# Two sums of weight quarters in a hybrid decoder block: from VectorE adds to adding transfers issued by GpSimd

## The chip, the cores and the metric

The kernel runs on one core of a Trainium2 chip. The metric is the device time of one execution in microseconds; lower is better. Five engines work side by side, each through its own queue in order: TensorE (PE; its weight loads are listed apart as PEld), VectorE (DVE), ScalarE (ACT), GpSimd (POOL) and SyncE (SP), which here issues most transfers between DRAM and the on-chip buffers. Semaphores tie the queues together.

## The reference, cut to what matters

One layer on 528 tokens (16 meta tokens and 512) of width 1024. The same normalised input `h` is projected by columns of one wide matrix `w_in`; a forgetting-attention (FoX) branch with 8 heads and an mLSTM branch with 4 heads are gated, merged and projected:

```
h = rms_norm(x, g_pre)
z = h @ w_in
(fq, fk, fv, ff, fz, mqk, mv, mi, mf, mo, mz, ga, gb) = split(z)
oa = forgetting_attention(fq, fk, fv, log_sigmoid(ff + b_fox_f))
ya = (oa * silu(fz)) @ w_a
...                                  # mLSTM branch: hb
yb = (hb * silu(mz)) @ w_b
merged = sigmoid(ga) * ya + sigmoid(gb) * yb
out = x + rms_norm(merged @ w_o, g_post)
```

All is float32. A matrix product is made from high and low parts of both factors (three products: high by high, high by low, low by high).

## The kernel before, in words

The four mLSTM heads come first, up to about 481 us of the profile; then the FoX branch in four pairs `p` of heads, with the gates `ga` and `gb` between them; then the merge and the output projection, from about 835 us.

Many projections are computed 256 columns at a time as a *unit* (`st_unit`) by a seven-product scheme on quarters: the weight block of 1024 rows by 256 columns is cut into quarters of 512 rows by 128 columns, the tokens likewise (`TB`, made once). Seven products of sums of quarters (X, Y, Z, W in `st_products`) take the place of eight. The unit's weights are made ready by `st_narrow`:

- SP loads two blocks of 512 KB: `r0` (rows 0 to 511) and `r1` (rows 512 to 1023). In each, `a` is the left 128 columns and `b` the right. They take two of the four buffers of the tag `raw`, which all weight loads of the kernel share in turn.
- The *a split*: the left half of `r0` (quarter a11) is split by `split` into a high part (ScalarE, L250) and a low part (VectorE, L252).
- VectorE adds in place: L263, left half of `r0` += right half of `r0` (the sum s3); L264, right half of `r0` += right half of `r1` (the sum s1).
- The *b split* of all of `r0` (s3 and s1), the *c split* of `r1` (a12 and a22), two more adds into `r1` (L269, L270: s2 and s4), and the *d split* of `r1`.

TensorE takes them in the order a (X), b (Y, Z), c (W, Y), d (X, Z), 12 matmuls each. In the profile a split's tiles are named after the unit and the letter: `wgb2b_h` and `wgb2b_l` are the high and low part of the b split of unit 2 of gate `gb`; its raw buffers appear as `wgb_r`. The units through `st_narrow` are: `mz` (8, in the mLSTM part) and, in the FoX part, `fq`, `fz`, `ga` and `gb`, 4 each, 16 in all. The projections `fk` (plain) and `fv` (`v_seven`, through `st_wide`) use other code.

Around them, `prob_part(p, m, ...)` makes one head's attention: TensorE makes scores `pl` in four row blocks; GpSimd adds a mask into a row of `ab` (L993); VectorE takes scores and `ab` to `lt` with the row minima `mn` (L1008), which frees the scores' bank; ScalarE exponentiates (L1013); VectorE inverts the row sum `rsum` (L1014); GpSimd (L1016) and VectorE (L1018) write the normalised row to `pn`. The tag of `lt` has two buffers. `ptr_part` transposes `pn` on TensorE (`pt`, `pmt`) and splits the result (`pth`, `ptl` at L1043 and L1044, `ptm`); `fout_part` multiplies by the values (`pfo`). `gb_part` multiplies `yb` by the gate on GpSimd (L974) and stores it through GpSimd's transfer queue (L975), which is all that queue carries.

The program is written in this order of parts, but a scheduler orders each engine's queue by its own estimates and places the semaphores; the order is fixed when the kernel is built. `behind` and `pin` hold a few instructions in place.

Of the kernel before, what the change touches and what calls it, by code (L numbers as in the profile page):

```python
# [12 lines left out]
ALU = mybir.AluOpType  # L13

P = 128
# [11 lines left out]
MV = 512  # L27
# [5 lines left out]
C_MO, C_MZ, C_GA, C_GB = 8208, 10256, 12304, 13328  # L33
# [20 lines left out]
def tile_hybrid_block(ctx: ExitStack, tc: tile.TileContext, x, meta, norm_pre, norm_post, w_in, b_fox_f,  # L54
                      conv_w, conv_b, b_i, b_f, g_head, w_a, w_b, w_o, out):
    nc = tc.nc
    V, S, G, T = nc.vector, nc.scalar, nc.gpsimd, nc.tensor
    x2, out2 = x[0], out[0]
    win, wa, wb, wo = w_in[0], w_a[0], w_b[0], w_o[0]
# [12 lines left out]
    def banks(name, n):  # L72

        return [psum1(f"{name}_{i}") for i in range(n)]
# [23 lines left out]
    def sb(shape, dt, tag, name, pool=None, **kw):  # L98

        n = 1  # L100
        for d in shape[1:]:
            n *= d
        size = BYTES.get(tag, 4096)
        t = (pool or wk).tile([shape[0], size // (2 if dt == BF16 else 4)], dt, tag=tag, name=name, **kw)[:, 0:n]
        if len(shape) == 3:
            t = t.rearrange("p (a b) -> p a b", a=shape[1])
        elif len(shape) == 4:
            t = t.rearrange("p (a b c) -> p a b c", a=shape[1], b=shape[2])
        return t
# [13 lines left out]
    def wload(src, k0, nk, c0, nc_, name):  # L123
        raws = []
        hk = 1024 // nc_
        for u in range(nk // hk):
            raw = wp.tile([P, hk, nc_], F32, tag="raw", bufs=4, name=f"{name}_r{u}")
            r0 = k0 + u * hk * P
            nc.sync.dma_start(raw, src[r0:r0 + hk * P, c0:c0 + nc_].rearrange("(k p) n -> p k n", p=P))
            raws.append(raw)  # L130
        return raws, hk, nc_, name
# [17 lines left out]
    def mm3(ps, ah, al, bh, bl, start, stop, **kw):  # L149
        T.matmul(ps, ah, bh, start=start, stop=False, **kw)  # L150
        T.matmul(ps, ah, bl, start=False, stop=False, **kw)  # L151
        T.matmul(ps, al, bh, start=False, stop=stop, **kw)  # L152
# [93 lines left out]
    def split(src, name, tags=("whi", "wlo"), pool=None, bufs=None, into=None):  # L246
        kw = {} if bufs is None else {"bufs": bufs}
        shape = [P, src.shape[1], src.shape[2]]
        hi = into[0] if into else (pool or wp).tile(shape, F32R, tag=tags[0], name=f"{name}_h", **kw)
        first = S.activation(hi, src, AF.Copy)  # L250
        lo = into[1] if into else (pool or wp).tile(shape, F32R, tag=tags[1], name=f"{name}_l", **kw)
        V.tensor_tensor(lo, src, f(hi), ALU.subtract)  # L252
        split.first = first
        return hi, lo

    def st_narrow(c0, name, into=None, late=None, first=None):

        (r0,), (r1,) = (wload(win, 512 * i, 4, c0, 256, f"{name}{i}")[0] for i in range(2))
        a, b = slice(0, P), slice(P, 2 * P)
        o = {"a11": split(r0[:, :, a], f"{name}a", ("whs", "wls"), mw, 1, into)}  # L260
        if first:
            behind(split.first, first)
        V.tensor_tensor(r0[:, :, a], r0[:, :, a], r0[:, :, b], ALU.add)  # L263
        V.tensor_tensor(r0[:, :, b], r0[:, :, b], r1[:, :, b], ALU.add)  # L264
        x, y = split(r0, f"{name}b")
        o["s3"], o["s1"] = (x[:, :, a], y[:, :, a]), (x[:, :, b], y[:, :, b])
        x, y = split(r1, f"{name}c")
        o["a12"], o["a22"] = (x[:, :, a], y[:, :, a]), (x[:, :, b], y[:, :, b])
        d = V.tensor_tensor(r1[:, :, b], r0[:, :, a], r1[:, :, b], ALU.add)  # L269
        V.tensor_tensor(r1[:, :, a], r1[:, :, a], r1[:, :, b], ALU.add)  # L270
        x, y = split(r1, f"{name}d")
        if late:
            behind(d, late[0])
            behind(split.first, late[1])
        o["s4"], o["s2"] = (x[:, :, a], y[:, :, a]), (x[:, :, b], y[:, :, b])
        return o
# [18 lines left out]
    def st_products(o, units, between=lambda i: None):  # L295


        begun = set()

        def prod(d, w, t):  # L300
            (wh_, wl_), (th, tl) = o[w], TB[t]
            for m, (wz, yx, _, ts) in enumerate(units):
                bank = wz if d in "WZ" else yx
                dst = bank[:, 0:256] if d in "WY" else bank[:, 256:512]
                first = (m, d in "WZ") not in begun
                begun.add((m, d in "WZ"))
                for k in range(4):
                    st, sp = first and k == 0, k == 3
                    if ts is None:
                        mm3(dst, wh_[:, k, :], wl_[:, k, :], th[:, k, :], tl[:, k, :], st, sp, skip_group_check=True)  # L310
                    else:
                        mm3(dst, th[:, k, ts], tl[:, k, ts], wh_[:, k, :], wl_[:, k, :], st, sp, skip_group_check=True)

        def halves(bank):
            return bank.rearrange("p (s n) -> p s n", s=2)

        prod("X", "a11", "b11")
        prod("Y", "s3", "t3")
        for wz, yx, snap, _ in units:
            S.activation(snap[:, 0:2], halves(yx), AF.Copy)  # L320
        between(0)
        prod("Z", "s1", "t1")
        prod("W", "a12", "b21")
        for wz, yx, snap, _ in units:
            S.activation(snap[:, 3], wz[:, 256:512], AF.Copy)
        prod("Y", "a22", "t4")
        between(1)
        prod("X", "s2", "t2")
        for wz, yx, snap, _ in units:
            st_products.copied = S.activation(snap[:, 2], yx[:, 256:512], AF.Copy)  # L330
        prod("Z", "s4", "b22")
        for wz, yx, snap, _ in units:
            V.tensor_tensor(yx[:, 256:512], snap[:, 0], yx[:, 256:512], ALU.subtract)
            V.tensor_tensor(halves(yx), halves(yx), snap[:, 2:4], ALU.subtract)
        for wz, yx, snap, _ in units:
            last = V.tensor_tensor(halves(wz), halves(wz), snap[:, 1:3], ALU.add)
        return last
# [33 lines left out]
    def behind(ins, other):  # L371

        tc.add_manual_dep(ins.ins, other.ins.name, mybir.DependencyInfo(
            mybir.DependencyClass.NoSync, mybir.DependencyReason.DATA), reason="behind")
        return ins
# [264 lines left out]
    a = gi  # L640
# [7 lines left out]
    for c in range(NCH):  # L648
        k0, k1 = NM + c * P, NM + (c + 1) * P
# [4 lines left out]
    for c in range(NCH):  # L654
        k0, k1 = NM + c * P, NM + (c + 1) * P
# [140 lines left out]
        mo_part.late = late  # L796
        return so

    def st_unit(c0, name, room, into=None, late=None, first=None):

        ps = banks(f"p{name}", 2)
        st_unit.added = st_products(st_narrow(c0, f"w{name}", into, late, first),
                                    [(ps[0], ps[1], room.rearrange("p a (b n) -> p (a b) n", b=2), None)])
        return ps

    def mz_part(h, u):
        g = sb([P, 2, SEQ], F32, ("qk1h", "qk1l")[u], f"gz{h}{u}")
        into = None
        if u:
            t = sb([P, 2, 4, P], F32R, "sg", f"wz{h}{u}a", gp)  # L810
            into = t[:, 0], t[:, 1]
        ps = st_unit(C_MZ + h * MV + u * 256, f"z{h}{u}", g, into, mo_part.late if h and not u else None)
        for m in range(2):
            mz_part.late = st_unit.added, S.activation(g[:, m, :], ps[m], AF.Sigmoid)
        for m in range(2):
            mi = 80 + h * 4 + u * 2 + m
            V.scalar_tensor_tensor(g[:, m, :], ps[m], gc[:, mi:mi + 1], g[:, m, :], ALU.mult, ALU.mult)
        return g
# [70 lines left out]
    for h in range(MH):  # L889
# [5 lines left out]
        k = conv_part(h, 1)  # L895
        if h:
            w = decay(h)
        if pend is not None:
            wb_part(pend[0], bt)
        if h == 0:  # L900
            v = v0
            ps = banks("pv01", 2)
# [4 lines left out]
            w = decay(0)  # L907
# [29 lines left out]
    def fk_part(p):  # L937
        w = wchunk(win, 0, KC, C_FK + p * 256, 256, f"wfk{p}")
        kh = sb([P, 2, L], F32R, "qk1h", f"fkh{p}")
        kl = sb([P, 2, L], F32R, "qk1l", f"fkl{p}")  # L940
        for m in range(2):
            ps = banks(f"pfk{p}{m}", 2)
            proj_t_all(ps, w, m)
            for u in range(2):
                hv = kh[:, m, u * HL:u * HL + HL]
                S.activation(hv, ps[u][:, 0:HL], AF.Copy)
                V.tensor_tensor(kl[:, m, u * HL:u * HL + HL], ps[u][:, 0:HL], f(hv), ALU.subtract)
        return kh, kl
# [130 lines left out]
    k = fk_part(0)  # L1079
# [3 lines left out]
    for p in range(FH // 2):  # L1083
        if p:
# [3 lines left out]
            k = fk_part(p)  # L1088
# [40 lines left out]
    for u in range(4):  # L1129
# [20 lines left out]
        if u < 2:  # L1150
            for i in range(2):
                b = 2 * u + i
# [11 lines left out]
    w = wchunk(wo, 0, KC, 0, 512, "wo_0")  # L1164
# [8 lines left out]
    for u in (2, 3):  # L1173
        w = wchunk(wo, 0, KC, u * 256, 256, f"wo{u}")
        for b in range(NCH):
            ps = psum1(f"pout{u}{b}")
# [40 lines left out]
```

## Time and profile before

| | |
|---|---|
| three runs | 928.32, 928.46, 929.09 us (median 928.46) |
| the profiled execution | 927.63 us, its span 925.8 us |
| TensorE, VectorE, ScalarE, GpSimd busy | 906.0, 730.4, 504.5, 117.5 us |
| TensorE's granted clock over the span | 0.999 |
| bytes by transfer | 97.54 MB; SP's queue 92.76 MB, GpSimd's queue 2.10 MB |

The span runs from the first to the last instruction. Busy times are of one execution; matmuls overlap each other and their ends are modelled, so a wait of TensorE is best read from the list of waits. A row of the timeline gives the start in us, the duration in us, engine, line, operation, output and inputs, and in brackets how long the engine had been idle before it and what ended that. A row of waits gives the engine and what waited, for whom, and then the sum in us, the number of times and the longest.

### The profile page before, as it was taken

To read this page: it belongs to the slowest core of one execution; us is meant where nothing else is said; L and a number is where in the kernel's file an instruction comes from. 1 tells how busy PE (TensorE), PEld (TensorE's weight loads), DVE (VectorE), ACT (ScalarE), POOL (GpSimd) and SP (SyncE) were. 2 spreads that over 40 slices of the span, in tenths; PEclk is the share of its full clock that TensorE was granted. 3 is DMA by queue.
4 is the path that set the end of the run, shared out by engine and by line. 5 is a ranking of instruction groups with operands and counts; after the bars stand their busy time and mean duration, and the time that the engine had idled before them with its cause. 6 is when DMAs were issued, how large, how long until landed. Compare 5 with 4: busy or idle time off the path is not lost.

```text
span 925.8 us, 16722 instructions
## 1 busy us (share of the span) xinstructions
PE 906.0 (98%) x6744; PEld 858.4 (93%) x6744; DVE 730.4 (79%) x1196; ACT 504.5 (54%) x860; POOL 117.5 (13%) x168
## 2 busy tenths in 40 slices
PE   8999899999999999999999999999999999999997
PEld 6998799899998999999999989999999999988887
DVE  6889688579887598876898866997896997985534
ACT  5646556545665456664565525565755665863231
POOL 3052000100101000000100002221333121300000
PEclk9999999999999999999999999999999999999999
DMA  7313143123331333231242442344342333258402
GB/s 233 94 50 103 46 134 91 40 69 92 117 112 57 92 91 90 95 103 51 95 114 69 124 128 73 95 123 137 100 142 81 102 112 121 87 203 300 140 18 91
DMA packets 78664, 97.54 MB, mean 105 GB/s; under 512 B 5237, under 2 KB 66773, under 8 KB 78586
## 3 DMA queue, kind: packets, MB, share of 16 engines
q1 hardware_dynamic: 76520, 92.76, 32.5%
q0 software_dynamic: 576, 2.10, 0.6%
q10 hardware_dynamic: 1490, 1.61, 0.5%
q8 instruction: 53, 0.87, 0.4%
q14 instruction: 25, 0.20, 0.1%
HBM read 90.62 MB, written 5.83 MB: 104 GB/s over the span
## 4 chain that ended last, share of the span: by engine, by line
PE 66%; DVE 22%; ACT 5%; issue 3%; DMA 2%; POOL 1%; DVEq 0%; POOLq 0%; ACTq 0%
PE pyb L151 3%; PE pyb L150 3%; PE pyb L152 3%; PE pz L150 3%; PE pz L152 3%; PE pz L151 3%; PE pqk L150 3%; PE pqk L152 3%; PE pqk L151 3%; PE pv L152 2%; PE pv L150 2%; PE pv L151 2%; PE pfk L150 2%; PE pfk L152 2%; PE pfk L151 2%
## 5 line engine op out<-in xcount | busy, mean ns | idle before, releaser
L151 PE MATMUL pyb<-bl,wb_h 128*128 128x512 f32 x128 | 49.8, 389 | 0.0
L152 PE MATMUL pyb<-bh,wb_l 128*128 128x512 f32 x128 | 49.8, 389 | 0.0
L150 PE MATMUL pyb<-bh,wb_h 128*128 128x512 f32 x128 | 49.8, 389 | 0.0
L1016 POOL TENSOR_SCALAR pn<-lt,rsum 128x128 f32<-128x128 f32 x32 | 30.4, 952 | 127.6 <-DVE rsum L1014 127.5
L732 DVE SCALAR_TENSOR_TENSOR y<-z,gc,y 128x512 f32<-128x512 f32 (+1 forms) x48 | 35.9, 754 | 2.1 <-ACT y L725 1.4
L150 PE MATMUL pfk<-hh,wfk_h 128*128 128x264 f32 x128 | 36.4, 285 | 0.0
L150 PE MATMUL pqk<-hh,wq_h 128*128 128x258 f32 x128 | 36.4, 284 | 0.0
L150 PE MATMUL pqk<-hh,wk_h 128*128 128x264 f32 x128 | 36.3, 284 | 0.0
L151 PE MATMUL pfk<-hl,wfk_h 128*128 128x264 f32 x128 | 36.3, 283 | 0.0
L152 PE MATMUL pqk<-hh,wk_l 128*128 128x264 f32 x128 | 36.3, 283 | 0.0
L152 PE MATMUL pfk<-hh,wfk_l 128*128 128x264 f32 x128 | 36.3, 283 | 0.0
L151 PE MATMUL pqk<-hl,wk_h 128*128 128x264 f32 x128 | 36.2, 283 | 0.0
L152 PE MATMUL pqk<-hh,wq_l 128*128 128x258 f32 x128 | 36.0, 282 | 0.0
L151 PE MATMUL pqk<-hl,wq_h 128*128 128x258 f32 x128 | 36.0, 282 | 0.0
L849 POOL TENSOR_TENSOR mrs<-mss,mhalf 128x1 f32<-128x1 f32 x16 | 9.2, 575 | 191.1 <-DVE mss L847 188.2
L993 POOL TENSOR_TENSOR ab<-ab,mask_q 128x128 f32<-128x128 f32 x32 | 27.0, 874 | 49.5 <-DVE vl L488 34.8
L144 DVE TENSOR_TENSOR wo_l<-wo_r,wo_h 128x1024 fp32r<-128x1024 f32 x12 | 15.7, 1313 | 16.9 <-ACT wo_h L142 16.9
L152 PEld LDWEIGHTS pyb<-bh,wb_l 128*128 128x128 f32 x128 | 24.0, 188 | 5.0
L150 PEld LDWEIGHTS pyb<-bh,wb_h 128*128 128x128 f32 x128 | 24.0, 188 | 4.9
L151 PEld LDWEIGHTS pyb<-bl,wb_h 128*128 128x128 f32 x128 | 24.0, 188 | 4.8
L884 DVE TENSOR_TENSOR yb<-pyb,yb 128x512 f32<-128x512 f32 x24 | 16.5, 686 | 13.9 <-PE pyb L152 13.9
L142 ACT ACTIVATE wo_h<-wo_r 128x1024 fp32r<-128x1024 f32 x12 | 12.7, 1059 | 24.4 <-PE pya L151 13.2
(2206 smaller groups left out, 3961.2 us busy)
## 6 DMA issues: line engine op xcount, KB each, us to landing
wv_r<-in_w_in_dram SPq DMA_DIRECT2D x16, 512.0 KB, 4.3
wo_r<-in_w_in_dram SPq DMA_DIRECT2D x16, 512.0 KB, 3.8
wz_r<-in_w_in_dram SPq DMA_DIRECT2D x16, 512.0 KB, 3.7
wb_r<-in_w_b_dram SPq DMA_DIRECT2D x16, 512.0 KB, 3.8
ab<-d_na SPq DMA_DIRECT2D x8, 672.0 KB, 4.5
wq_r<-in_w_in_dram SPq DMA_DIRECT2D x8, 512.0 KB, 3.7
wk_r<-in_w_in_dram SPq DMA_DIRECT2D x8, 512.0 KB, 3.6
wfq_r<-in_w_in_dram SPq DMA_DIRECT2D x8, 512.0 KB, 3.7
```

The source lines that it names most:

```text
L142: pin(S.activation(hi, raw, AF.Copy))
L144: pin(V.tensor_tensor(lo, raw, f(hi), ALU.subtract))
L150: T.matmul(ps, ah, bh, start=start, stop=False, **kw)
L151: T.matmul(ps, ah, bl, start=False, stop=False, **kw)
L152: T.matmul(ps, al, bh, start=False, stop=stop, **kw)
L732: V.scalar_tensor_tensor(y[:, t0:L], z[:, m, t0 + j:L + j], gc[:, j * 16 + mi:j * 16 + mi + 1], y[:, t0:L], ALU.mult, ALU.add)
L849: G.tensor_tensor(rs, ss, mhalf, ALU.pow)
L884: V.tensor_tensor(dst, ps[i], dst, ALU.add)
L993: G.tensor_tensor(ab[:, o:o + P], ab[:, o:o + P], mask_q, ALU.add)
L1016: G.tensor_scalar(pn[:, o:o + P].rearrange("p (g t) -> p g t", g=4), lt[:, 0:32].unsqueeze(1).to_broadcast([P, 4, 32]), rsum, None, ALU.mult)
```

## The change

In 16 of the 24 units, those of the FoX part, the sums s3 and s1 are no longer made by VectorE from `r0` and `r1`. GpSimd issues four transfers from DRAM, 256 rows by 128 columns each, that add the right quarters of `w_in` into `r0` in place: two into its right half (`b`, from rows 512 on) and then two into its left half (`a`, from rows 0 on). The right half needs only the load of `r0`; the left half also needs the a split to have read a11. The b split waits for all four. The mLSTM's `mz` units keep the adds.

```
-    def st_narrow(c0, name, into=None, late=None, first=None):
+    def st_narrow(c0, name, into=None, late=None, first=None, fetched=True):
...
-        V.tensor_tensor(r0[:, :, a], r0[:, :, a], r0[:, :, b], ALU.add)
-        V.tensor_tensor(r0[:, :, b], r0[:, :, b], r1[:, :, b], ALU.add)
+        if fetched:
+
+            for dst, k0 in ((b, 512), (a, 0)):
+                for i in range(2):
+                    rows = win[k0 + 256 * i:k0 + 256 * i + 256, c0 + P:c0 + 2 * P]
+                    G.dma_start(r0[:, 2 * i:2 * i + 2, dst], rows.rearrange("(k p) n -> p k n", p=P), accum_op=ALU.add)
+        else:
+            V.tensor_tensor(r0[:, :, a], r0[:, :, a], r0[:, :, b], ALU.add)
+            V.tensor_tensor(r0[:, :, b], r0[:, :, b], r1[:, :, b], ALU.add)
...
-    def st_unit(c0, name, room, into=None, late=None, first=None):
+    def st_unit(c0, name, room, into=None, late=None, first=None, fetched=True):
...
-        ps = st_unit(C_MZ + h * MV + u * 256, f"z{h}{u}", g, into, mo_part.late if h and not u else None)
+        ps = st_unit(C_MZ + h * MV + u * 256, f"z{h}{u}", g, into, mo_part.late if h and not u else None,
+                     fetched=False)
```

Lines after this place move down by 7 and more; line numbers in this document are those of before unless a row of after is shown. The scheduler orders the queues anew. Three places follow; a row has line, operation, output and inputs, with the buffers' numbers.

**GpSimd, around the third `gb` unit** (wgb2, in the second pair of heads: `pn` of head 2). Before:

```order
L974 TENSOR_TENSOR yb<-yb,sgb_7059 128x1024
L975 DMA d_yb_5802<-yb 128x1024
L1016 TENSOR_SCALAR pn_7442<-lt_7466,rsum_7469 128x128
L1016 TENSOR_SCALAR pn_7442<-lt_7474,rsum_7477 128x128
L1016 TENSOR_SCALAR pn_7442<-lt_7482,rsum_7485 128x128
L1016 TENSOR_SCALAR pn_7442<-lt_7490,rsum_7494 128x128
```

After; `wgb_r_7725` is r0 of wgb2, `wfz_r_7513` of the unit fz1, `wfq_r_7893` of the unit fq2:

```order
L983 DMA d_yb_5802<-yb 128x1024
L268 DMA wfz_r_7513<-in_w_in_dram 128x2x128 x4
L268 DMA wgb_r_7725<-in_w_in_dram 128x2x128 x2
L268 DMA wfq_r_7893<-in_w_in_dram 128x2x128 x2
L1024 TENSOR_SCALAR pn_7454<-lt_7478,rsum_7481 128x128
L1024 TENSOR_SCALAR pn_7454<-lt_7486,rsum_7489 128x128
L268 DMA wgb_r_7725<-in_w_in_dram 128x2x128
L1024 TENSOR_SCALAR pn_7454<-lt_7494,rsum_7497 128x128
L268 DMA wgb_r_7725<-in_w_in_dram 128x2x128
L1024 TENSOR_SCALAR pn_7454<-lt_7502,rsum_7506 128x128
```

Eight fetches of three units stand between the store of `yb` and the first pn of the head; the last two fetches of wgb2, which go into the left half, stand on either side of the third pn.

**VectorE, around the same unit's b and c split.** Before:

```order
L252 TENSOR_TENSOR wgb2b_l<-wgb_r_7711,wgb2b_h 128x1024
L1014 RECIPROCAL rsum_7494<-rsum_7494 128x1
L1018 TENSOR_SCALAR pn_7442<-lt_7490,rsum_7494 128x512
L252 TENSOR_TENSOR wgb2c_l<-wgb_r_7713,wgb2c_h 128x1024
L333 TENSOR_TENSOR pfz_1_7500<-yb,pfz_1_7500 128x256
L269 TENSOR_TENSOR wgb_r_7713<-wgb_r_7711,wgb_r_7713 128x4x128
L334 TENSOR_TENSOR pfz_1_7500<-pfz_1_7500,yb 128x512
L336 TENSOR_TENSOR pfz_0_7499<-pfz_0_7499,yb 128x512
L1044 TENSOR_TENSOR ptl_7620<-pt_7623,pth_7619 128x2x256
L1044 TENSOR_TENSOR ptl_7620<-pt_7630,pth_7619 128x3x128
L270 TENSOR_TENSOR wgb_r_7713<-wgb_r_7713 128x4x128
L1008 ISA lt_7675,mn_7676<-pl_7653,ab_7649 128x144
```

After:

```order
L1026 TENSOR_SCALAR pn_7454<-lt_7502,rsum_7506 128x512
L252 TENSOR_TENSOR wgb2b_l<-wgb_r_7725,wgb2b_h 128x1024
L252 TENSOR_TENSOR wgb2c_l<-wgb_r_7727,wgb2c_h 128x1024
L340 TENSOR_TENSOR pfz_1_7512<-yb,pfz_1_7512 128x256
L276 TENSOR_TENSOR wgb_r_7727<-wgb_r_7725,wgb_r_7727 128x4x128
L341 TENSOR_TENSOR pfz_1_7512<-pfz_1_7512,yb 128x512
L343 TENSOR_TENSOR pfz_0_7511<-pfz_0_7511,yb 128x512
L1052 TENSOR_TENSOR ptl_7634<-pt_7637,pth_7633 128x2x256
L1052 TENSOR_TENSOR ptl_7634<-pt_7644,pth_7633 128x3x128
L1052 TENSOR_TENSOR ptl_7634<-pt_7649,pth_7633 128x4x128
L1016 ISA lt_7689,mn_7690<-pl_7667,ab_7663 128x144
```

L263 and L264 are gone; the b split has moved behind the row's last pn and stands with the c split ahead of all that leads to the next head's row minima; of `ptl` all three splits now come ahead of these, and the second add into `r1` (L270, now L277) has moved behind them.

**ScalarE, around the third `fq` unit** (wfq2). Before:

```order
L250 ACTIVATE wfq2b_h<-wfq_r_7877 128x1024
L330 ACTIVATE sgb_7708<-pgb_1_7710 128x256
L250 ACTIVATE wfq2c_h<-wfq_r_7879 128x1024
L967 ACT_TABLE_LOAD
L967 ACTIVATE sgb_7708<-pgb_0_7709 128x512
L967 ACTIVATE sgb_7708<-pgb_1_7710 128x512
L1043 ACTIVATE pth_7844<-pt_7848 128x2x256
L1043 ACTIVATE pth_7844<-pt_7855 128x3x128
L1043 ACTIVATE pth_7844<-pt_7860 128x4x128
L1045 ACTIVATE ptm_7846<-pmt_7847 128x512
L320 ACTIVATE fqs_7874<-pfq_1_7876 128x512
L250 ACTIVATE wfq2d_h<-wfq_r_7879 128x1024
```

After:

```order
L337 ACTIVATE sgb_7722<-pgb_1_7724 128x256
L250 ACTIVATE wfq2b_h<-wfq_r_7893 128x1024
L975 ACT_TABLE_LOAD
L975 ACTIVATE sgb_7722<-pgb_0_7723 128x512
L975 ACTIVATE sgb_7722<-pgb_1_7724 128x512
L1051 ACTIVATE pth_7860<-pt_7864 128x2x256
L1051 ACTIVATE pth_7860<-pt_7871 128x3x128
L1051 ACTIVATE pth_7860<-pt_7876 128x4x128
L1053 ACTIVATE ptm_7862<-pmt_7863 128x512
L250 ACTIVATE wfq2c_h<-wfq_r_7895 128x1024
L327 ACTIVATE fqs_7890<-pfq_1_7892 128x512
L250 ACTIVATE wfq2d_h<-wfq_r_7895 128x1024
```

The high part of the c split, wfq2c_h, stood right behind that of the b split and the gate's copy; now it follows the gate's sigmoids and the splits of the transposed weights.

More of the change, by code (lines that the diff above doesn't have):

```diff
@@ L797, in mo_part @@
         return so
-    def st_unit(c0, name, room, into=None, late=None, first=None):
+    def st_unit(c0, name, room, into=None, late=None, first=None, fetched=True):
         ps = banks(f"p{name}", 2)
-        st_unit.added = st_products(st_narrow(c0, f"w{name}", into, late, first),
+        st_unit.added = st_products(st_narrow(c0, f"w{name}", into, late, first, fetched),
                                     [(ps[0], ps[1], room.rearrange("p a (b n) -> p (a b) n", b=2), None)])
```

## The prediction

> **What bounds the kernel now.** I read the page first, then the windows of the changed stretch, then TensorE's waits there, then the timelines around them.
>
> ```profile
> span 925.8 us, 16722 instructions
> PE 906.0 (98%) x6744; PEld 858.4 (93%) x6744; DVE 730.4 (79%) x1196; ACT 504.5 (54%) x860; POOL 117.5 (13%) x168
> ```
> ```profile
> 481.00:835.00 354.00, 349.38 (x2790) 339.44 (x2790) 296.21 (x516) 206.98 (x351) 67.66 (x72) 1.00 0.37 116
> ```
>
> The windows row reads: length, busy PE, PEld, DVE, ACT, POOL, granted clock, DMA share. The 16 changed units all lie in 481 to 835 us. TensorE is busy 349.38 of 354 us there at full clock, so VectorE's 296.21 us matter only where TensorE runs out of prepared operands. The waits of the weight loads in that stretch show where:
>
> ```profile
> PEld pl L150 <- DVE fvl L488: 2.1, 2, 1.6
> PEld pfq L152 <- DVE wfq2d_l L252: 0.8, 1, 0.8
> PEld pga L152 <- DVE wga3d_l L252: 0.8, 1, 0.8
> PEld pgb L150 <- DVE mn L1008: 0.7, 1, 0.7
> PEld pga L150 <- DVE mn L1008: 0.7, 1, 0.7
> PEld pga L152 <- DVE wga3b_l L252: 0.6, 1, 0.6
> PEld pgb L152 <- DVE wgb3d_l L252: 0.6, 1, 0.6
> PEld pgb L152 <- DVE wgb1d_l L252: 0.6, 1, 0.6
> ```
>
> Together 6.9 us, all behind VectorE: that is about all the change can win. But the same rows say that VectorE and TensorE are in step at eight places, so there any new lateness of VectorE goes through in full.
>
> **The change, part by part.** Removed: two adds in each of 16 units.
>
> ```profile
> L263 DVE TENSOR_TENSOR wgb_r<-wgb_r x4: 667/677/683, 538.5 to 737.3; 128x512 f32<-128x512 f32 x4
> L264 DVE TENSOR_TENSOR wgb_r<-wgb_r,wgb_r x4: 678/685/692, 539.7 to 738.1; 128x512 f32<-128x512 f32 x4
> L975 POOL DMA_DIRECT2D d_yb<-yb x4: 620/620/780, 572.8 to 760.4; - x4
> L993 POOL TENSOR_TENSOR ab<-ab,mask_q x32: 447/784/1447, 452.3 to 790.6; 128x128 f32<-128x128 f32 x32
> d_yb<-yb POOLq DMA_DIRECT2D x4, 512.0 KB, 3.2
> yb<-in_conv_w_dram SPq DMA_DIRECT2D x1, 32.0 KB, 2.0
> wv_r<-in_w_in_dram SPq DMA_DIRECT2D x16, 512.0 KB, 4.3
> ```
>
> 32 adds of 0.68 us are 21.8 us off VectorE. Added: 64 fetches of 128 KB (256 rows of 128 floats), issued by GpSimd, which add into the buffer. No row of before shows an adding transfer, so both prices are bounded. Issue: GpSimd's only transfers take 0.62 to 0.78 us; from above, GpSimd's mask adds take 0.447 us at best and 1.447 where they meet other work, so 1.0 us more, 1.6. I take 0.8, the slowest issue seen, as each fetch has twice the pieces. Landing, counted from issue: between the 32 KB row, 2.0, and the largest plain loads, 4.3; I take 2.8, between 2.0 and the 3.2 of GpSimd's own 512 KB stores, because 128 KB lies between them. GpSimd gains 64 x 0.8 = 51 us over its 117.5; it stays far from full, and its bytes (8.4 MB more on 97.5, at a DMA share of 0.37) I cost at nothing: the loads they meet are issued well ahead of use.
>
> In place of 1.36 us on VectorE, a sum now takes: the low half of the first quarter done, third fetch issued, fourth fetch issued, landing. The first two fetches go into the other half and need only the load, so they are early. Of the 16 splits of the sums (the "b" splits), TensorE's list names one, wga3b_l; the nearest others are these:
>
> ```profile
> 609.17 1.21 DVE L252 TENSOR_TENSOR wgb1b_l<-wgb_r,wgb1b_h 128x1024 fp32r<-128x1024 f32 x1
> 613.05 0.28 PE L150 MATMUL pgb<-t3h,wgb1b_h 128*128 128x256 f32 x1
> 801.10 0.69 DVE L252 TENSOR_TENSOR wga2a_l<-wga_r,wga2a_h 128x512 fp32r<-128x512 f32 x1
> 806.04 1.22 DVE L252 TENSOR_TENSOR wga2b_l<-wga_r,wga2b_h 128x1024 fp32r<-128x1024 f32 x1
> 808.74 0.28 PE L150 MATMUL pga<-t3h,wga2b_h 128*128 128x256 f32 x1
> ```
>
> wga2: third and fourth fetch follow each other once the low half is done: 801.8 + 0.8 + 2.8 = 805.4, high part (1.06, below) to 806.5, 0.4 later than now, with a lead of 1.5 to TensorE's use at 808.74. wgb1 (and wgb3) have a lead of 2.7. All these I cost at nothing; landing over 4 us would use the cover up. The first two fetches stand in GpSimd's queue ahead of pn's and can hold them for two issues, 1.6 us, or until their load is there; pn's readers are transposes, and no row of TensorE's list names POOL, so that lateness costs nothing either. SP's next loads wait for the buffers' last readers, which come later only where named below.
>
> Four places have no lead.
>
> **Third output gate (wgb2) and second attention gate (wga1).** The third and fourth fetch stand in GpSimd's queue on either side of a pn, and VectorE's queue now has the b split directly ahead of everything up to the next row minima (L1008), whose bank TensorE waits for.
>
> ```profile
> 649.89 0.69 DVE L252 TENSOR_TENSOR wgb2a_l<-wgb_r,wgb2a_h 128x512 fp32r<-128x512 f32 x1
> 649.92 2.29 POOL L1016 TENSOR_SCALAR pn<-lt,rsum 128x128 f32<-128x128 f32 x2 [0.79 <-DVE rsum L1014]
> 653.06 1.06 ACT L250 ACTIVATE wgb2b_h<-wgb_r 128x1024 fp32r<-128x1024 f32 x1 [1.75 <-DVE wgb_r L264]
> 656.09 1.23 DVE L252 TENSOR_TENSOR wgb2c_l<-wgb_r,wgb2c_h 128x1024 fp32r<-128x1024 f32 x1
> 657.23 0.42 DVE L333 TENSOR_TENSOR pfz<-yb,pfz 128x256 f32<-128x256 f32 x1
> 661.02 0.30 DVE L1008 CUSTOM_DVE_ANT_0 lt<-pl,ab 128x144 f32<-128x144 f32 x1
> 661.74 0.39 PE L150 MATMUL pgb<-hh,wgb2a_h 128*128 128x256 f32 x1 [0.46 <-DVE mn L1008]
> 781.55 0.69 DVE L252 TENSOR_TENSOR wga1a_l<-wga_r,wga1a_h 128x512 fp32r<-128x512 f32 x1
> 781.58 2.29 POOL L1016 TENSOR_SCALAR pn<-lt,rsum 128x128 f32<-128x128 f32 x2 [0.79 <-DVE rsum L1014]
> 788.89 0.42 DVE L333 TENSOR_TENSOR pfz<-yb,pfz 128x256 f32<-128x256 f32 x1
> ```
>
> wgb2: the low half ends at 650.6. GpSimd is through the first of its two pn at 651.1 (half of 2.29), issues the third fetch to 651.9, does the second pn to 653.0, issues the fourth, which lands at 655.8. ScalarE's high part takes 1.06, to 656.9. Then VectorE's two lows, 1.14 from start to start (656.09 to 657.23): 659.2, where pfz started at 657.23. So +1.9 us. From there to L1008 the queue holds as many instructions as before (a ptl has taken the place of L270), so L1008 and the gate's first product come 1.9 later; nothing on TensorE stands between. In a formula: landing + issue - 1.7. wga1 is the same place two heads on: 781.58 + 1.15 + 0.8 + 1.15 + 2.8 + 1.06 + 2.28 = 790.8 against 788.89, +1.9.
>
> **Third query projection (wfq2).**
>
> ```profile
> 669.43 0.69 DVE L252 TENSOR_TENSOR wfq2a_l<-wfq_r,wfq2a_h 128x512 fp32r<-128x512 f32 x1
> 671.03 1.21 POOL L1016 TENSOR_SCALAR pn<-lt,rsum 128x128 f32<-128x128 f32 x1 [2.14 <-DVE rsum L1014]
> 674.96 1.28 ACT L967 ACT_TABLE_LOAD   x1 [1.06 <-DVE pgb L336]
> 678.55 0.64 ACT L1045 ACTIVATE ptm<-pmt 128x512 fp32r<-128x512 f32 x1
> 680.04 0.28 PE L152 MATMUL pfq<-hh,wfq2c_l 128*128 128x256 f32 x1
> ```
>
> Third fetch at 670.1, when the low half is done; pn; fourth fetch at 670.1 + 0.8 + 1.2 = 672.1, landing at 674.9, high part to 676.0, so the table load behind it starts 1.0 late. The c split now stands behind ptm on ScalarE: the row of ScalarE's work from 674.96 to 679.19 (4.23) comes first, then 1.06 for wfq2c_h: 681.3, and 1.14 for the low: 682.4. TensorE wants wfq2c_l at 680.04: +2.4, of which 1.0 is the fetch and 1.4 the new order. The 0.8 behind wfq2d_l stays.
>
> **Fourth attention gate (wga3).**
>
> ```profile
> 816.16 0.68 DVE L252 TENSOR_TENSOR wga3a_l<-wga_r,wga3a_h 128x512 fp32r<-128x512 f32 x1
> 819.29 1.04 ACT L250 ACTIVATE wga3b_h<-wga_r 128x1024 fp32r<-128x1024 f32 x1
> ```
>
> 816.84 + 0.8 + 2.8 = 820.4 for the fourth landing, where wga3b_h started at 819.29: 1.1 later, of which the 0.8 behind wga3d_l is won back, as VectorE has two adds less in front of it. +0.3.
>
> **Won.** The 1.2 us behind wgb1d_l and wgb3d_l go: there the last sums now stand ahead of the transposed weights' splits, and four adds less precede them. Of the 2.1 behind fvl I take 1.4: the stretch loses a wait for the second load and the 0.69 add, but TensorE's own last product may bind. Together -2.6.
>
> Sum: 1.9 + 1.9 + 2.4 + 0.3 - 2.6 = +3.9 us. The profiled execution takes 927.63, 0.83 under the median 928.46; on its own time 931.5, on the median 932.4.
>
> At the low ends (issue 0.62, landing 2.0) the terms are 0.9, 0.9, 1.4, -1.0, and -3.3 won: -1.1, 927.4. At the high ends (1.6, 4.3): 4.2, 4.2, 4.7, 2.0, and -1.0 won: +14, 942.5.
>
> [...]
>
> **Rivals.** *Faster.* The mechanism: the b split no longer needs the second load, nor VectorE. It decides where landing + issue stay under 2.2: then wgb2 and wga1 cost 0.5 each, wfq2's new order must find its c split early, and wga3 (-1.0) and the 3.3 above are won: 925.2. For it speaks that 6.9 us wait on VectorE; against it that GpSimd's own transfers already add up to 3.8 from issue to landing if 0.62 stands in front of 3.2. *Hidden.* Gains and waits cancel within 1.9 us (0.2%, about what a measurement can tell from no change): the low ends, 927.4. *Starved issue.* GpSimd is slowed by VectorE at each issue as its mask adds are (0.447 to 1.447): the high ends, 938 to 943. [...]
>
> **Numbers.** The forecast with waits of 1 to 3 us at wgb2, wga1 and wfq2: 0.45. Starved: 0.13. Hidden: 0.22. Faster: 0.20. Slower by over 0.2% is 0.45 + 0.13. Time 932.4. 926 to 941 leaves out about 0.12 below and 0.05 above; the forecast's own range is 930.4 to 938.
>
> **What would show it.** In the profile after, VectorE's busy time falls by 22 us and GpSimd's issue rows read 0.6 to 1.6 us; ScalarE waits for a DMA at wgb2b_h, wga1b_h, wfq2b_h and wga3b_h; TensorE's waits behind L1008 grow from 0.7 to over 2 each, one behind wfq2c_l is new, and those behind wgb1d_l and wgb3d_l are gone. I am wrong if the fetches land in under 1.5 us from issue, or if TensorE's waits of the stretch fall below 6.9 us.

## The result, and the profile after

1049.12 us (median of 4 runs) against 928.66 for the kernel before on the same chip: ratio 1.131, 95% interval 1.128 to 1.134. The forecast was 932.4, slower by some 4 us with a range to 941; the sign was right, the size wrong by a factor of about 30. The profiled execution took 1049.53 us. Line numbers from here on are those of the changed kernel. The page's first lines and the windows row of the changed stretch, which now ends about 957 instead of 835:

```profile
span 1047.8 us, 16888 instructions
PE 946.6 (90%) x6744; PEld 893.2 (85%) x6744; DVE 712.2 (68%) x1164; ACT 501.9 (48%) x860; POOL 180.9 (17%) x232
```
```profile
481.00:957.00 476.00, 389.63 (x2795) 373.63 (x2794) 279.43 (x486) 205.82 (x352) 131.86 (x136) 0.90 0.44 104
```

The stretch is 122 us longer, and that is the whole loss. In the row, TensorE stands idle for 86 us of it (5 before), and the same matmuls take 40 us longer (389.63 busy instead of 349.38), at a granted clock of 0.90 instead of 1.00. VectorE has less to do, as meant. GpSimd is busy 131.86 of 476 us, and yet it is what everything waits for, because it stands still between the fetches (L268). Its own rows, and then what L268 as a whole waited for:

```profile
676.10 1.21 POOL L268 DMA_DIRECT2D wfz_r<-in_w_in_dram  x1 [6.00 <-issue]
679.96 1.20 POOL L268 DMA_DIRECT2D wfz_r<-in_w_in_dram  x1 [2.65 <-issue]
683.78 1.20 POOL L268 DMA_DIRECT2D wfz_r<-in_w_in_dram  x1 [2.62 <-issue]
687.65 1.20 POOL L268 DMA_DIRECT2D wgb_r<-in_w_in_dram  x1 [2.67 <-issue]
```
```profile
  issue: 123.6, 43
```
```profile
wfq_r<-in_w_in_dram POOLq DMA_DIRECT2D x16, 128.0 KB, 3.6
```

"issue" is time in which the engine waits for nothing that the profile shows: no semaphore, no other engine. The fetches start 3.8 to 3.9 us apart, and over all 64 no two start closer than 3.76, although an issue takes 1.2 and nothing of the program holds the next one. 3.6 us is the time from issue to landing. So each fetch starts only when the one ahead of it has landed: 48 of the 64 start 0.26 to 0.34 us after that landing, and none sooner. pn, the mask adds and the stores stand behind the fetches in the same queue. Over 43 fetches the standing still is 123.6 us. Seven of the largest waits of the weight loads in the stretch, to be read against the 6.9 us in the prediction:

```profile
PEld pmt L1045 <- POOL pn L1024: 17.4, 4, 6.8
PEld pl L150 <- DVE ptl L1052: 12.6, 2, 7.0
PEld pl L150 <- ACT fkh L954: 12.5, 2, 6.5
PEld pga L150 <- ACT wga3b_h L250: 4.8, 1, 4.8
PEld pfz L150 <- ACT yb L327: 4.5, 2, 2.5
PEld pfq L150 <- ACT fqs L327: 4.4, 2, 2.2
PEld pfq L150 <- ACT wfq2b_h L250: 2.9, 1, 2.9
```

Two of the four places of the prediction are here by their own names (wga3b_h, wfq2b_h). The other two, wgb2 and wga1, are the row behind ptl. In TensorE's own list these four are 19.2 us of the 81 that it stands idle longer over the whole span. The two other large rows, pn and fkh, are places that the prediction took to cost nothing: pn waits behind the fetches in GpSimd's queue, and fkh stands in ScalarE's queue behind the b splits of wfz1 and wfz3, for whose fetches ScalarE waits 14.2 and 13.6 us. The first, among those who waited for L268:

```profile
  ACT wfz1b_h L250: 14.2, 1
```

wgb2 from the low half's end to the next head's scores, in the rows of GpSimd, ScalarE, VectorE and TensorE:

```profile
704.46 1.24 POOL L268 DMA_DIRECT2D wgb_r<-in_w_in_dram  x1 [0.28 <-issue]
705.29 1.07 POOL L1024 TENSOR_SCALAR pn<-lt,rsum 128x128 f32<-128x128 f32 x1
711.46 1.23 POOL L268 DMA_DIRECT2D wgb_r<-in_w_in_dram  x1 [5.10 <-issue]
```
```profile
715.47 1.06 ACT L250 ACTIVATE wgb2b_h<-wgb_r 128x1024 fp32r<-128x1024 f32 x1 [8.87 <-issue]
716.55 1.23 DVE L252 TENSOR_TENSOR wgb2b_l<-wgb_r,wgb2b_h 128x1024 fp32r<-128x1024 f32 x1 [9.52 <-ACT wgb2b_h L250]
```
```profile
699.92 0.28 PE L151 MATMUL pfz<-t1l,wfz1b_h 128*128 128x256 f32 x1
...
721.70 0.59 PE L150 MATMUL pl<-fkh,fqh 128*128 128x264 f32 x1 [6.70 <-DVE ptl L1052]
722.09 0.42 PE L151 MATMUL pl<-fkl,fqh 128*128 128x264 f32 x1
...
723.18 0.41 PE L150 MATMUL pgb<-hh,wgb2a_h 128*128 128x256 f32 x1
```

The order is the one that the prediction walked through: third fetch, pn, fourth fetch, high part, low part. But the fourth fetch starts 7.0 us behind the third, where the prediction had 1.9: the third takes 6.7 us to land here, beside a load of 672 KB (see the experiment on that load). ScalarE and VectorE stand 9 us at the b split with everything behind it, and TensorE 6.7. Then comes the second loss: a matmul of 256 columns takes 0.41 us instead of 0.28. The trace's record of the granted clock has 17 pieces of 3.4 to 10.2 us at half clock in this stretch, 99.0 us in all, among TensorE's waits; the kernel before has none between its start and its last 4 us. The pieces are 3.4, 6.8 or 10.2 us long. How long a wait has to be before one follows is not shown; in the run below with wgb1 and wgb3 alone, waits of 2.5 and 2.8 us are each followed by a piece.

### The profile page after: what moved, and what is told of

The parts are those of the page before. It is cut to its first block, busy times and chain, and to the rows that moved or that the text cites. A ratio compares the mean times of both kernels' runs of the same rounds, so it can differ in the third digit from the quotient of the medians.

```text
span 1047.8 us, 16888 instructions
## 1 busy us (share of the span) xinstructions
PE 946.6 (90%) x6744; PEld 893.2 (85%) x6744; DVE 712.2 (68%) x1164; ACT 501.9 (48%) x860; POOL 180.9 (17%) x232
## 4 chain that ended last, share of the span: by engine, by line
PE 43%; DVE 21%; issue 15%; DMA 9%; ACT 6%; POOL 6%; POOLq 0%; DVEq 0%; ACTq 0%; SPq 0%
DMA wfz_r<-in_w_in_dram 3%; PE pqk L150 2%; PE pqk L152 2%; PE pqk L151 2%; PE pyb L151 2%; PE pyb L150 2%; PE pyb L152 2%; PE pz L150 2%; PE pz L152 2%; PE pz L151 2%; DMA wgb_r<-in_w_in_dram 2%; DMA wfq_r<-in_w_in_dram 2%; POOL pn L1024 2%; PE pv L152 2%; PE pv L150 2%
## 5 line engine op out<-in xcount | busy, mean ns | idle before, releaser
L150 PE MATMUL pl<-fkh,fqh 128*128 128x264 f32 (+3 forms) x40 | 15.8, 395 | 27.1 <-ACT fkh L954 12.1
L1024 POOL TENSOR_SCALAR pn<-lt,rsum 128x128 f32<-128x128 f32 x32 | 34.1, 1114 | 31.0 <-DVE rsum L1022 31.0
L150 PEld LDWEIGHTS pl<-fkh,fqh 128*128 128x128 f32 x40 | 10.1, 252 | 29.1 <-DVE ptl L1052 12.6
L268 POOL DMA_DIRECT2D wfz_r<-in_w_in_dram x16 | 19.4, 1214 | 73.6 <-DMA wfz_r<-in_w_in_dram 36.7
L1021 ACT ACTIVATE lt<-lt,mn 128x144 f32<-128x144 f32 (+3 forms) x32 | 18.2, 570 | 27.8 <-DVE mn L1016 27.8
L1016 DVE CUSTOM_DVE_ANT_0 lt<-pl,ab 128x144 f32<-128x144 f32 (+3 forms) x32 | 13.3, 435 | 26.8 <-POOL pn L1024 26.4
L268 POOL DMA_DIRECT2D wga_r<-in_w_in_dram x16 | 19.5, 1219 | 64.2 <-issue 29.3
L268 POOL DMA_DIRECT2D wgb_r<-in_w_in_dram x16 | 19.6, 1223 | 54.5 <-issue 26.7
```

Of the source, the lines that this page charges most:

```text
L268: G.dma_start(r0[:, 2 * i:2 * i + 2, dst], rows.rearrange("(k p) n -> p k n", p=P), accum_op=ALU.add)
L1016: V.tensor_tensor_reduce(out=lt[:, s0:s1], in0=ps, in1=ab[:, OFFA[c] + s0:OFFA[c] + s1], op0=ALU.add, op1=ALU.min, scale=1.0, scalar=3e38 ...
L1021: S.activation(lt[:, 0:kn], lt[:, 0:kn], AF.Exp, bias=mn[:, li:li + 1], scale=-1.0, accum_out=rsum)
L1024: G.tensor_scalar(pn[:, o:o + P].rearrange("p (g t) -> p g t", g=4), lt[:, 0:32].unsqueeze(1).to_broadcast([P, 4, 32]), rsum, None, ALU.mult)
```

## The experiments

The theory: GpSimd can start a fetch only when there is room for it in a scratch whose size the program sets, here called the ring, and the kernel makes this ring small. One line that the change does not touch sets the size, `dynamic_dma_scratch_size=1024`. The rivals: adding transfers go one at a time whatever the room; the adding itself is slow; the lateness comes from pn behind the fetches; or the loss is elsewhere. All runs, with the idle time of TensorE (span less busy time) and the sum of the half-clock pieces after 481 us (us; without the piece at each run's end), from each profiled execution:

| run | us | before on that chip | TensorE idle | TensorE busy | half clock |
|---|---|---|---|---|---|
| before | 928.66 | | 19.8 | 906.0 | 0 |
| changed | 1049.12 | 928.66 | 101.2 | 946.6 | 99.0 |
| scratch 1152 | 982.09 | 927.66 | 52.2 | 928.0 | 37.5 |
| scratch 2048 | 971.33 | 928.13 | 49.9 | 920.6 | 27.3 |
| 128-row fetches | 996.09 | 928.13 | 64.4 | 930.7 | 54.6 |
| plain fetches | 948.86 | 928.13 | 32.4 | 914.8 | 17.1 |
| pn on VectorE, 1024 | 1045.24 | 928.13 | 101.8 | 941.0 | 102.4 |
| pn on VectorE, 2048 | 967.42 | 927.65 | 44.8 | 919.3 | 20.5 |
| small ab load, 2048 | 967.01 | 927.65 | 44.1 | 921.2 | 23.9 |
| two units, 1024 | 937.26 | 927.65 | 27.0 | 907.4 | 10.2 |
| five units, 2048 | 941.29 | 927.65 | 27.3 | 911.9 | 6.8 |
| wgb1 and wgb3, 2048 | 938.99 | 927.66 | 26.3 | 912.4 | 13.7 |
| the same, yb's product on VectorE | 932.12 | 927.66 | 23.7 | 907.3 | 0 |
| wfz0, wfz2, wgb0, 2048 | 927.36 | 927.66 | 18.3 | 907.4 | 0 |

**Twice the ring.**

```
-    nc = _bacc.Bacc("TRN2", ..., dynamic_dma_scratch_size=1024)
+    nc = _bacc.Bacc("TRN2", ..., dynamic_dma_scratch_size=2048)
```

> The changed kernel with GpSimd's descriptor scratch at 2048 bytes a partition instead of 1024; the instructions and their order are the same on every engine. In the changed kernel the 64 fetches never start less than 3.76 us apart, although the issue takes 1.2. Room theory (a fetch cannot be written before the one ahead has left a ring that holds less than two of them): with twice the room the next fetch follows 1.2 to 1.5 us behind the first, though a third or fourth may still wait; a unit's four fetches take some 6 to 10 us instead of 15 to 17, and the time falls to 935 to 975. Order theory (adding fetches into one buffer, or their semaphores, let one fly at a time whatever the room): spacing stays at 3.8, time 1045 to 1057. Loss-elsewhere theory (the late sums cost little, the clock fell for another reason): spacing falls, time stays above 1000.

971.33 us, ratio 1.047 (1.043 to 1.050). The room theory holds: 78 of the 120 us go with that one number. GpSimd's rows at wfz1, where three of the four fetches now go out together:

```profile
639.26 3.65 POOL L268 DMA_DIRECT2D wfz_r<-in_w_in_dram  x3 [5.27 <-DVE wfk_l L144]
645.93 1.20 POOL L268 DMA_DIRECT2D wfz_r<-in_w_in_dram  x1 [3.02 <-issue]
```

**A little more ring.** The same edit with 1152.

> The changed kernel with GpSimd's descriptor scratch at 1152 bytes a partition instead of 1024, 12% more; the order is the same on every engine. [...]

With two fetches in flight the time should lie between the 1049 of the changed kernel and the 971 with 2048 (the author's estimate was 975 to 1005); if it moved in proportion to the size, some 12% of the way, it should be 1035 to 1045.

982.09 us, ratio 1.058 (1.056 to 1.061): 12% more room takes back 67 us, so it is a step and not a slope. The same place:

```profile
647.38 2.44 POOL L268 DMA_DIRECT2D wfz_r<-in_w_in_dram  x2 [5.29 <-DVE wfk_l L144]
653.87 2.43 POOL L268 DMA_DIRECT2D wfz_r<-in_w_in_dram  x2 [4.06 <-issue]
```

**Smaller fetches.**

```
-                for i in range(2):
-                    rows = win[k0 + 256 * i:k0 + 256 * i + 256, c0 + P:c0 + 2 * P]
-                    G.dma_start(r0[:, 2 * i:2 * i + 2, dst], rows.rearrange("(k p) n -> p k n", p=P), accum_op=ALU.add)
+                for i in range(4):
+                    G.dma_start(r0[:, i, dst], win[k0 + P * i:k0 + P * i + P, c0 + P:c0 + 2 * P], accum_op=ALU.add)
```

> The changed kernel with each fetch cut in two: 8 adding fetches of 128 rows (64 KB) for a unit instead of 4 of 256, same scratch of 1024 bytes. Room theory: each takes half the room, so two or three fly at once; issue about 0.7 each, a unit's eight take 8 to 11 us instead of 15 to 17, time 960 to 1005. One-at-a-time theory (one adding fetch in flight whatever its size): eight times some 3 us, 24 us or more for a unit, time 1100 to 1200.

996.09 us, ratio 1.073 (1.070 to 1.076). "One at a time" falls: three go out 0.54 apart, the fourth waits.

```profile
652.09 2.65 POOL L267 DMA_DIRECT2D wfz_r<-in_w_in_dram  x3 [5.02 <-DMA wfz_r<-in_w_in_dram]
656.94 0.89 POOL L267 DMA_DIRECT2D wfz_r<-in_w_in_dram  x1 [2.20 <-issue]
```

**Fetches that do not add.** `accum_op=ALU.add` taken out, so that the fetched quarter overwrites and the two sums are not made.

> The changed kernel with the 64 fetches as plain loads of the same bytes to the same places in the same order (leaves out the two sums' adding: the fetched quarter overwrites instead). Room theory where an adding fetch takes two read entries for each piece: a plain one takes half, so two or three fit, spacing 1.2 to 2, time 935 to 975. Room theory where both take the same entries: spacing 3 to 3.9 and 1020 to 1050. Adding theory (the adding itself, read, add and write, is what takes 3.6 us to land): landing falls to 2.5 or less, spacing falls with it by 1 us or more even if still one at a time, time 960 to 1010.

948.86 us, ratio 1.022 (1.019 to 1.025). Three fly at once in the ring of 1024, as with 2048 when adding, and landing is quicker: 2.5 us at least and 3.0 in the median over all transfers into wgb's raw buffers (SP's loads among them), where with adding in the ring of 2048 these are 3.4 and 4.1. So adding takes more room, and it lands later. The shortest times from a fetch's start to the start of the first, second and third fetch behind it:

| run | next | second next | third next | so in flight |
|---|---|---|---|---|
| changed (1024) | 3.76 | 7.67 | 11.5 | 1 |
| 1152 | 0.71 | 3.79 | 5.08 | 2 |
| 2048 | 0.70 | 1.45 | 3.77 | 3 |
| 128 rows (1024) | 0.54 | 1.07 | 2.85 | 3 |
| plain (1024) | 0.69 | 1.42 | 3.74 | 3 |

In each of these runs a fetch that finds the ring full starts 0.25 to 0.34 us after a landing: that of the first fetch ahead of it in the changed kernel, of the second with 1152, and of the third in the other three. So the size of the ring sets how many fly.

An estimate from the last column, if all of the set size serves the fetches: an adding fetch of 256 rows takes more than 512 of it (two do not fly with 1024) and at most 576 (two fly with 1152). One of 128 rows, and a plain one of 256 rows, take 257 to 341 (three fly with 1024, a fourth does not). That GpSimd stands still with as many in flight as that is in the "issue" rows.

**pn off GpSimd.**

```
-            G.tensor_scalar(pn[:, o:o + P].rearrange(...
+            V.tensor_scalar(pn[:, o:o + P].rearrange(...
```

> The changed kernel with the 32 pn (the softmax's first block times the reciprocal sum) on VectorE instead of GpSimd; fetches as they are. It parts the loss in two: what the fetches cost by being late themselves, and what they cost by standing ahead of pn in GpSimd's queue. If pn behind the fetches is most of it (TensorE waits 16.4 us for pn, VectorE 26.4 and ScalarE through it 27.8): 980 to 1010. If the late b splits alone set the time: 1035 to 1050. VectorE takes on 32 times some 0.3 us, 10 us, which it has room for.

> The changed kernel with scratch 2048 and pn on VectorE, so that GpSimd's queue holds only fetches, mask adds and the stores. Queue theory (pn behind waiting fetches is most of what is left with the wider ring: VectorE waits 13.6 us for pn's buffer there): 945 to 958. Lateness theory (the third and fourth fetch land too late whatever stands beside them): 965 to 972, as with the narrow ring, where the same edit gained only 4 us.

1045.24 and 967.42 us, each 4 less than with pn on GpSimd; the changed kernel's own runs lie between 1045.6 and 1056.8, so at 1024 this is hardly a gain. TensorE's largest wait of the changed kernel, for pn, is a symptom. In TensorE's own list it is 16.4 us; with pn on VectorE that row is gone, 9.6 us stand behind VectorE's pn instead, and the wait behind ptl grows from 11.9 to 20.5. The late sums themselves set the time.

**The load beside the last fetches.** With 2048:

```
-        ab = sb([P, NA], F32, "ab", f"ab{h}", gp)
-        nc.sync.dma_start(ab, d_na[h:h + 1, :].to_broadcast([P, NA]))
+        ab = prob_part.ab = prob_part.ab if h else sb([P, NA], F32, "ab", "ab0", gp)
+        nc.sync.dma_start(ab[0:16 if h else P], d_na[h:h + 1, :].to_broadcast([16 if h else P, NA]))
```

> The changed kernel with scratch 2048, and ab (the additive mask of a head, 672 KB) loaded into 16 of 128 partitions only for all heads but the first (84 KB; the others keep the first head's values); the order on every engine is the same. Collision theory: at wgb2 and wga1 the third and fourth fetch land 6 to 7 us after issue because the ab load starts beside them; without its bytes they land in 3.6 to 4.5, the two waits of 7.0 to 7.3 us before the row of products pl fall to 4 to 5, no clock is lost there, and the time falls from 971 by 5 to 12 us. Latency theory (adding fetches land so late by themselves): waits and time within 2 us of 971.

967.01 us: 4.3 less than with the full load, just under the range given. The landings and the waits are as expected; the half clock is not, as it stays at 23.9 us of 27.3. The landings around wgb2, first with the full load and then with the small one (KB, us from issue to landing), and TensorE's waits there, in the same order:

```profile
ab<-d_na SPq DMA_DIRECT2D x1, 672.0 KB, 6.0
wgb_r<-in_w_in_dram POOLq DMA_DIRECT2D x2, 128.0 KB, 5.1
```
```profile
wgb_r<-in_w_in_dram POOLq DMA_DIRECT2D x2, 128.0 KB, 3.9
ab<-d_na SPq DMA_DIRECT2D x1, 84.0 KB, 2.6
```
```profile
PE pl L150 <- DVE ptl L1052: 14.0, 2, 7.2
```
```profile
PE pl L150 <- DVE ptl L1052: 7.7, 2, 4.0
```

With this ring the collision costs 3.1 us at each of wgb2 and wga1. There the fourth fetch and the load of ab start within 0.1 us of each other (664.40 and 664.44, 817.75 and 817.81). Being in flight together is not enough: in the changed kernel the load slows the third fetch of wgb2, which starts 1.0 us ahead of it (6.7 us to land), but at wga1 the fetches start 1.4 us ahead and 2.5 behind it and land in 3.6. What sets the limit was not tried.

**Two units alone.** In this run and in all that follow the adds stay on VectorE but for the units named:

```
-        if fetched:
+        if name in ("wgb2", "wga1"):
```

> The kernel before with the sums fetched at two units alone, wgb2 and wga1 (8 fetches, scratch 1024 as before); all others add on VectorE. The prediction gave +1.9 us to each of the two: 932. With what the changed kernel showed: 4 fetches 3.8 us apart, the last two behind pn and beside the 672 KB load of ab, so the row minima wait 5 to 7 us at each place (6.86 and 5.40 in the changed kernel) and TensorE's clock is halved for 3.4 to 6.8 us after each (half of it lost): 942 to 950. If the loss of the changed kernel comes only from fetches of several units crowding GpSimd, a lone unit costs little: 928 to 933.

937.26 us, ratio 1.011 (1.009 to 1.013), +9.6 where the prediction gave these two +3.8. Lone units, with no others in GpSimd's queue, pay most of the price:

```profile
PE pl L150 <- DVE ptl L1052: 9.5, 2, 5.2
```

4.8 us for each, and 10.2 us of half clock behind them. It came out 5 us under the range that was given from the changed kernel (942 to 950). One reason is on record: that range had the last two fetches beside the load of ab as in the changed kernel, and here those of wgb2 land in 3.5 and 3.7 us, although that load is under way.

**Five units with lead.** Scratch 2048; fetched at wfz1, wfz3, wgb0, wgb1 and wgb3.

> Scratch 2048, and the sums fetched only at wfz1, wfz3, wgb0, wgb1 and wgb3, where the b split kept 3.7 to 8.5 us of lead to TensorE's use in the changed kernel with scratch 2048; the other 11 units add on VectorE. Lead theory (a late sum costs only where the lead is shorter than the fetches take): no new wait on TensorE, the 0.6 behind wgb1d_l and wgb3d_l may go: 925.5 to 928.8. Crowding theory (any fetch on GpSimd delays pn and so the softmax): 932 to 945.

941.29 us, ratio 1.015 (1.013 to 1.016). The lead theory falls in this form: no b split of these five is late (3.7 to 10.3 us ahead of TensorE's use), and still 13.6 us are lost. The longest wait is in a unit that fetches nothing:

```profile
PE pfq L150 <- ACT fqs L327: 5.0, 2, 2.5
```

**Where that wait is from.** Only wgb1 and wgb3 fetched, and then the same with the product of yb and its gate (L982) on VectorE.

```
-        G.tensor_tensor(y, y, sg, ALU.mult)
+        V.tensor_tensor(y, y, sg, ALU.mult)
```

> Scratch 2048, and the sums fetched only at wgb1 and wgb3 (leads of 2.7 us, which the prediction called enough). Order theory from the run with five units: their fetches are in time, but VectorE's queue behind them is in another order, so that the second add of wfq1 and wfq3 runs beside GpSimd's multiplication of yb and takes 2.6 us instead of 0.7, fqs on ScalarE stands behind it, TensorE waits 2.5 us there and its clock is halved for 3.4 us: 933 to 937. If they are free, 926.5 to 928.5, and the loss of that run came from wfz1 and wfz3.

> The same as the run with wgb1 and wgb3 alone, but the multiplication of yb by its gate (4 times) on VectorE instead of GpSimd. Collision theory: the second add of wfq1 and wfq3 takes 0.7 us again, the two waits for fqs shrink below 1.5 us or go, and the clock stays full; 4 to 8 us less than with wgb1 and wgb3 alone, unless the 4 multiplications of some 1.2 us on VectorE take part of it back. If the waits are the order's alone: the same time within 1.5 us, or more.

938.99 us, ratio 1.011 (1.010 to 1.013), a little over the range, and 932.12, ratio 1.0045 (1.003 to 1.006), within the range. The scheduler puts wfq1's two adds later in VectorE's queue once wgb1's adds are gone. In the first run GpSimd and VectorE do this (two rows), in the second VectorE does both:

```profile
628.71 2.40 POOL L982 TENSOR_TENSOR yb<-yb,sgb 128x1024 f32<-128x1024 f32 x1 [12.01 <-ACT sgb L975]
629.05 2.60 DVE L277 TENSOR_TENSOR wfq_r<-wfq_r 128x512 f32<-128x512 f32 x1
```
```profile
628.11 1.21 DVE L982 TENSOR_TENSOR yb<-yb,sgb 128x1024 f32<-128x1024 f32 x1
629.25 0.68 DVE L277 TENSOR_TENSOR wfq_r<-wfq_r 128x512 f32<-128x512 f32 x1
```

The add takes 2.60 us beside GpSimd's product and 0.68 alone. In the kernel before the same product meets the low part wfq1d_l, which takes 2.58 instead of 1.2 and has 1.9 us of lead; now it meets an add that ScalarE waits for, with fqs behind. TensorE's waits there, first and second run:

```profile
PE pfq L150 <- ACT fqs L327: 5.3, 2, 2.8
```
```profile
PE pfq L150 <- ACT fqs L327: 1.6, 2, 0.9
```

The half-clock pieces at these two places (10.2 us) go with them. The pair is not quite clean: in the second run ScalarE's queue also has fqs one instruction earlier, ahead of a split of 1.0 us, so the collision is 1.9 us of the move and the order the rest. The 4.5 us that are left to the kernel before lie in many small waits, of which the largest is the 1.6 us above; they were not parted.

**Three units with nothing behind the fetch.** Scratch 2048; wfz0, wfz2 and wgb0.

> Scratch 2048, and the sums fetched only at wfz0, wfz2 and wgb0, where ScalarE came to the high part of the b split 9 to 12 us after the low half of the first quarter in the kernel before, so that ScalarE's and VectorE's queues have nothing behind the fetch; TensorE's order is that of before. Queue theory (a fetch costs where an in-order engine stands at its landing with other work behind it): no wait is new, 926.5 to 929. Order theory (any move of VectorE's adds costs here): 931 or more.

927.36 us (10 runs), ratio 1.0004 (0.999 to 1.002): no change that can be measured, as the queue theory had it. ScalarE reaches wfz0b_h at 586.0 and waits for TensorE, not for the fetch:

```profile
586.01 1.06 ACT L250 ACTIVATE wfz0b_h<-wfz_r 128x1024 fp32r<-128x1024 f32 x1 [1.26 <-PE pfvm L481]
```

So fetched sums can be hidden, and then they bring nothing, as VectorE was not late there either. Nothing in the runs points to a version faster than the kernel before.

## Why the prediction was right or wrong

- **What bounds the kernel, and the bound on the gain: right.** TensorE's waits in the stretch came to 6.9 us, no run got clear below the kernel before, and TensorE had no cover at the places named. Lateness did go through in full.
- **Issue and landing of one fetch: right.** 0.8 us taken for the issue; where the ring has room, the next instruction of GpSimd follows 0.70 to 0.83 behind (the row reads 1.2, as it overlaps the next). Landing 2.8 taken, 3.6 measured in the median, within the bounds of 2.0 to 4.3; beside other loads single fetches took up to 6.9.
- **The step that failed: the fetches following one another.** Every term of the sum had "third fetch, fourth fetch, landing" with 0.8 us for each issue. They come 3.8 apart, because with a ring of 1024 one adding fetch is in flight at a time. A unit's four fetches take some 15 us (three times 3.85 and 3.6) instead of 5 (three times 0.8 and 2.8); at wgb2 and wga1 TensorE loses 6.7 and 5.2 us instead of 1.9, and at wga3b_h 4.6 instead of 0.3. At wfq2 it loses 2.7 behind the b split, where the prediction had 2.4 behind the c split (wfq2c_l), which did not come late. "GpSimd stays far from full" was read from its busy share, and a ring is not in that share: GpSimd is 17% busy in the changed kernel and holds up all others. The trace of before could not show the limit, with four stores in that queue 52 to 79 us apart; the line with 1024 stood in the kernel's text and went unread.
- **Cover elsewhere: wrong for the same reason.** "Landing over 4 us would use the cover up": from the low half's end, it took 11.5 us at wgb2; TensorE waits 1.1 us for wga2b_h, whose lead was 1.5, while at wgb1 and wgb3 TensorE itself came so late that the splits were in time. Waits for pn did reach TensorE, 16.4 us, where the prediction costed them at nothing, and so did the wait of ScalarE at wfz1 and wfz3: TensorE loses 12.1 us behind fkh, although these two b splits themselves were in time for TensorE.
- **Bytes at nothing: wrong at some places.** With the ring of 2048 the load of ab costs 3.1 us at each of wgb2 and wga1; in the changed kernel it makes one fetch of wgb2 land in 6.7 us, and wga1 goes free.
- **Won 2.6: half right.** The waits behind wgb1d_l and wgb3d_l went, as said; of the 2.1 behind fvl nothing was won, as they are 3.7 in the changed kernel. But the new order put an add of wfq1 and wfq3 beside GpSimd's product: in the changed kernel the first add into `r1` (L276, 2.28 us instead of 0.68), and TensorE waits 2.0 us twice for fqs; with wgb1 and wgb3 alone the second (L277), 2.7 us twice, and the clock behind it. That the order of the other units moves was seen, its price was not looked for.
- **A term that was missing: the clock.** No wait was priced above its own length. In the eight runs of the table with over 10 us more idle time than before, each us of it came with 0.4 to 0.7 us of longer matmuls (40.6 for 81.4 in the changed kernel, 14.6 for 30.1 with 2048).
- **VectorE's busy time** fell by 18.2 us, not 22: some of what stays on it runs slower; which part, is open.
- **The rivals.** Starved issue did not occur: the 64 issues took 1.19 to 1.42 us, and none the 1.6 of the high ends. That a full ring might stop GpSimd was not among the rivals.
- **The ends of the range.** One of the prediction's side sums does not come out. At the low and high ends its own rows give wga3 -0.6 and +2.6 (816.84 + 0.62 + 2.0 and 816.84 + 1.6 + 4.3, against 819.29, less the 0.8 won), not -1.0 and 2.0, so the ends are -0.7 and +14.7. The slip does not bear on the miss.
- **The sign** came out right, for the reason given at the four places, but three quarters of the idle time lies elsewhere.

What stays open: 971 against 949 us between adding and plain fetches is put down to the later landing (1 us) and to the ring (three in flight in both), but the two were not parted.

## What to carry to other kernels

Before moving work onto transfers that GpSimd issues, measure how many of them are in flight at once. Here that number set their spacing: 3.8 us with one in flight, although an issue took 1.2, and 0.7 with up to three. An engine's busy share says nothing of how long its queue stands still: GpSimd was 17% busy here and stood still for 123.6 us. A sum that moves from an engine to a transfer is latency in every queue that waits for it; in these runs it cost nothing only where nothing stood behind it (927.36 us with wfz0, wfz2 and wgb0). In the eight runs with over 10 us more idle time than before, a us of it cost 1.4 to 1.7 us with the longer matmuls; price a wait of TensorE in this kernel so until a trace says otherwise.

## What the runs showed of the hardware

- With one adding fetch in flight at a scratch size of 1024, two at 1152 and three at 2048, GpSimd stood still ahead of the next one, until 0.25 to 0.34 us after a landing, and the profile names that wait "issue": in the changed kernel 123.6 us over 43 fetches.
- At 1024 one adding fetch was in flight and three plain ones of the same shape: by the estimate above, over 512 of the size against at most 341. The adding one shows 272 packets and the plain one 48 (17408 and 3072 over 64 fetches), and it lands about 1 us later (3.4 against 2.5 at the least).
- 1152 instead of 1024 took the time from 1049 to 982 us.
- A wait of TensorE of 2.5 us was followed by 3.4 us at half clock (wfq1 with wgb1 and wgb3 fetched: the wait ends at 634.2, and the piece starts at 634.3).
